# A hybrid attention / RG-LRU block on one core: the opening's loads reordered, weights in 1 KB packets, nine products of zeros first, and the whole order replaced by another

## The chip, the core and the metric

The kernel runs on one core of one Trainium2 chip. Five engines work side by side: TensorE (PE in the views, its weight loads PEld), VectorE (DVE), ScalarE (ACT), GpSimd (POOL) and SyncE (SP), which here issues all DMAs. The metric is the device time of one execution in microseconds. Before the change it is 1078.18 us, the median of 3 runs (1078.18 to 1078.38).

## The reference, cut to what matters

```python
h = rms_norm(x, norm1_g)                      # x: 1024 tokens x 1024
proj = h @ w_in                               # 1024 x 2560: q, k, v, xl, gl, 512 columns each
q, k = rms_norm(q per head), rms_norm(k per head)       # 8 heads of 64
z = q @ k.T / 8                               # causal, strictly below the diagonal
w = sigmoid(z) * prod over later keys of sigmoid(-z)    # stick-breaking weights
attn = w @ v
xl = causal_depthwise_conv(xl)                # 4 taps
lru = rg_lru(xl) * gelu(gl)                   # 2 gates of 8 blocks of 64 x 64, a scan over 1024 tokens
x = x + concat(attn, lru) @ w_out
x = x + square(relu(rms_norm(x) @ w_up)) @ w_down       # 1024 -> 4096 -> 1024
```

## The kernel before, in words

Everything is f32 and held to nearly f32 accuracy by splitting: an operand a becomes a high part (a copy in the reduced f32 format that TensorE takes at full rate, made on ACT) and a low part (a minus the high part, made on DVE or POOL), and a product is three matmuls, low x high, high x low, high x high, added in PSUM.

The program has a front (norm, projections, attention, recurrence, output projection) and an MLP. The MLP saves products by Strassen-like sums of blocks; its matmuls write the banks `p`, `pa`, `pb`, `pc`.

No engine's order is written by hand. `record_front` and `record_mlp` record operations, each with an engine, a cost in ns and the tiles that it reads and writes. The front's operations belong to units, and the string list `ORDER` sets the order of the units: `I` loads the weights `q0` and the transposed input's first half (tokens 0 to 511, `ch` 0), `Xbc` loads two of the eight 128-row blocks (`kc`) of the transposed input (its high and low parts are `hTh` and `hTl`) for half `c`, `Wq1` and the like load weights, `St` loads two 128-token rows of `x` and squares them for the norm, `Rc` spreads the norm's factors over partitions (four transposes into `prs`), `Qpc`, `Vpc`, `Lpc` project, `Gp` normalises q and k (products `ss`, transposes `sst` and `rb`), `Apc` and `Dpc` are attention blocks of head pair p, `B`, `M`, `O`, `U` load and split `w_out` and its input and multiply them, `N`, `H`, `Y`, `Z` prepare the MLP. `Plan.schedule` then plays the recorded operations with a small model of the engines and DMAs, always taking the ready operation with the lowest priority number (the unit's place plus `BIAS` of its kind), and emits them in that order. `ALT` lists, by unit and place in it, the operations that go to their second engine (DVE or POOL, ACT or DVE) instead of their first. So the two tables and `ORDER` settle what stands where in each engine's queue, and an engine runs its queue strictly in that order on the chip.

What the steps below use:

- **The opening.** `xload` loads 128 x 512 of the transposed input, 256 KB, `wload` 128 x 256 of `w_in`, 128 KB. A `q` weight tile holds 128 columns of q and the same 128 of k, which lie 512 columns apart in `w_in`, so each partition gets two pieces of 512 bytes; the `v` tiles are one piece of 1 KB. `q0` uses 8 weight tiles and 8 input tiles for its first half. Each tile goes through ACT (high part: `hTh`, or `wq` with the norm's gain) and DVE or POOL (low part). Then `chain` runs 24 matmuls, 3 for each `kc`, for k and as many for q (`pq001`, `pq000` are k and q of the first half, `pq011`, `pq010` of the second): 48 products of 128x512 for each half.
- **The rows of `x` for the norm** (`sunit`): eight loads of 512 KB into two buffers (tag `A`, `COUNT` 2), squared with a row sum on ACT (`x<-x`, 128x1024), then a few small operations on DVE and a power on POOL (`rstd`).
- **DMA issue.** All loads go through SP in order; eight semaphores (`DMAHW0` to `DMAHW7` in the rows) take turns, so SP issues the ninth load only when the first has landed.
- **The transposes of attention weights**: 128x128 blocks of `w` go through TensorE into `pw`, a PSUM tile of which there is only one (`COUNT` pw=1); ACT or DVE copies it to `wt` before the next four transposes can write `pw`. Then `av` multiplies `wt` with v.
- **The products `w <- w, G`** finish the attention weights (on DVE, or on POOL by `ALT`).
- `warm(n)` existed already but stood in no unit of `ORDER`: n matmuls of a tile of zeros (`zb`, bf16) into a PSUM tile that nobody reads.

Of the kernel before, what the change touches and what calls it, by code (L numbers as in the profile page):

```python
# [1336 lines left out]
```

## Time and profile before

| what | value |
|---|---|
| median of 3 runs | 1078.18 us |
| the profiled execution: its own time | 1078.43 us |
| its span, first to last instruction | 1076.3 us |
| PE busy | 1055.7 us (98%), 5304 matmuls |
| DVE busy | 814.2 us (76%) |
| ACT busy | 575.2 us (53%) |
| POOL busy | 463.4 us (43%) |
| DMA | 120.81 MB, mean 112 GB/s |
| TensorE clock granted, mean | 0.999 |

How to read the views. "busy" is the union of an engine's instructions; a matmul's end is modelled, so neighbours overlap, and what a matmul costs in a dense row is the distance from its start to the next one's. "idle before, releaser" is the time in which the engine did nothing just before an instruction, and what ended it. In a windows view each row gives, for a stretch of the span, the busy time of PE, PEld, DVE, ACT and POOL with their counts, then the granted clock, the share of the DMA engines' time in use, and GB/s. Helper classes issue every instruction, so nearly all rows carry one line number (L1200), and rows are told apart by their tiles: `out<-in`.

### The profile page before, as it was taken

The page shows a single profiled execution, that of the slowest core. Times are in us where ns is not written, and L with a number is a line of the kernel's source. Part 1 is how long each engine was busy: PE and PEld are TensorE (multiplying, and loading weights), DVE is VectorE, ACT ScalarE, POOL GpSimd, SP SyncE. Part 2 cuts the span into 40 slices and gives each one's busy share as a digit, 9 for nine tenths or more (in the row PEclk, how much of TensorE's full clock was granted, in tenths as well). Part 3 has the DMA queues.
Part 4 walks back from the last instruction along what each step waited for, and adds up shares of the span by engine and source line. Part 5 has one row for each costly group of instructions (what it writes and reads, how often), then busy time and mean ns, then how long its engine had stood idle before and what let it go on. Part 6 is the DMA issues. An engine that isn't in the chain of part 4 may idle for free.

```text
span 1076.3 us, 14935 instructions
## 1 busy us (share of the span) xinstructions
PE 1055.7 (98%) x5304; PEld 853.1 (79%) x5304; DVE 814.2 (76%) x1093; ACT 575.2 (53%) x1023; POOL 463.4 (43%) x367
## 2 busy tenths in 40 slices
PE   6999999999999999999999999999999999999998
PEld 4888777769777777788888888888888888888886
DVE  6587877977977885674768888888666659788983
ACT  7754586775576644355227763444443368644431
POOL 2413011113024221267678434557665475742474
PEclk9999999999999999999999999999999999999999
DMA  9402110211117410053443253645343433435662
GB/s 301 155 15 59 31 55 30 64 40 60 33 47 276 164 41 1 21 165 99 135 130 98 89 175 119 186 140 172 105 125 115 129 93 121 117 120 175 199 202 89
DMA packets 80634, 120.81 MB, mean 112 GB/s; under 512 B 9136, under 2 KB 29104, under 8 KB 80560
## 3 DMA queue, kind: packets, MB, share of 16 engines
q1 hardware_dynamic: 80560, 119.86, 35.4%
q8 instruction: 42, 0.69, 0.2%
q14 instruction: 32, 0.26, 0.1%
HBM read 107.77 MB, written 12.06 MB: 111 GB/s over the span
## 4 chain that ended last, share of the span: by engine, by line
PE 90%; DVE 4%; ACT 3%; DMA 2%; issue 1%; SPq 0%; DVEq 0%; ACTq 0%
PE p L1200 28%; PE pa L1200 16%; PE pb L1200 8%; PE po L1200 8%; PE pq L1200 6%; PE pv L1200 4%; PE pc L1200 4%; PE pxl L1200 3%; PE pgl L1200 3%; PE pw L1200 3%; PE av L1200 3%; PE z L1200 2%; ACT x L1200 1%; DMA x<-in_x_dram 1%; DVE G L1200 1%
## 5 line engine op out<-in xcount | busy, mean ns | idle before, releaser
L1200 PE MATMUL pq<-hTh,wq 128*128 128x512 f32 x256 | 87.5, 406 | 11.5 <-DVE wq L1200 9.7
L1200 DVE TENSOR_TENSOR U<-p,U 128x512 f32<-128x512 f32 x80 | 54.7, 687 | 57.4 <-PE p L1200 56.9
L1200 PE MATMUL p<-m1t,st 128*128 128x512 f32 x384 | 89.9, 389 | 0.0
L1200 PE MATMUL p<-m0t,st 128*128 128x512 f32 x384 | 89.7, 389 | 0.0
L1200 PEld LDWEIGHTS p<-m1t,st 128*128 128x128 f32 x384 | 72.0, 188 | 15.1 <-POOL st L1200 0.2
L1200 PEld LDWEIGHTS p<-m0t,st 128*128 128x128 f32 x384 | 72.1, 188 | 14.9
L1200 DVE COPY wt<-pw 128x512 f32<-128x512 f32 (+1 forms) x80 | 50.3, 629 | 29.5 <-PE pw L1200 27.3
L1200 PEld LDWEIGHTS pq<-hTh,wq 128*128 128x128 f32 x256 | 49.1, 192 | 24.6 <-DVE wq L1200 9.7
L1200 PE MATMUL p<-m0b,sb 128*128 128x512 f32 x288 | 67.5, 390 | 0.0
L1200 PE MATMUL p<-m1b,sb 128*128 128x512 f32 x288 | 67.4, 389 | 0.0
L1200 PEld LDWEIGHTS p<-m1b,sb 128*128 128x128 f32 x288 | 54.1, 188 | 11.2
L1200 PEld LDWEIGHTS p<-m0b,sb 128*128 128x128 f32 x288 | 53.9, 188 | 11.1
L1200 ACT ACTIVATE G<-z,qv 128x512 f32<-128x512 f32 (+3 forms) x96 | 49.3, 579 | 25.0 <-PE z L1200 14.1
L1200 ACT ACTIVATE U<-U 128x512 f32<-128x512 f32 x97 | 57.3, 627 | 6.1 <-DVE U L1200 5.2
L1200 ACT ACTIVATE w<-z,qv 128x512 f32<-128x512 f32 (+3 forms) x96 | 48.2, 591 | 17.7 <-PE pw L1200 17.5
L1200 DVE TENSOR_TENSOR_SCAN G<-G,K 128x769 f32<-128x769 f32 (+3 forms) x32 | 47.9, 1507 | 5.4 <-ACT G L1200 4.2
L1200 PE MATMUL pq<-hTl,wq 128*128 128x512 f32 x128 | 50.8, 397 | 0.0
L1200 PEld LDWEIGHTS pw<-ident,w 128*128 128x128 f32 x288 | 34.1, 140 | 20.3 <-DVE wt L1200 6.2
L1200 PE MATMUL pv<-wv,hTh 128*128 128x256 f32 x256 | 49.6, 288 | 0.0
L1200 PE MATMUL pw<-ident,w 128*128 128x128 f32 x288 | 46.1, 278 | 2.3 <-DVE wt L1200 2.3
L1200 POOL MEMSET G<- 128x2 f32 x32 | 3.1, 101 | 104.6 <-DVE w L1200 60.4
L1200 PE MATMUL po<-woh,mxl 128*128 128x512 f32 x112 | 47.0, 420 | 1.0 <-DVE mxl L1200 1.0
(268 smaller groups left out, 2879.2 us busy)
## 6 DMA issues: line engine op xcount, KB each, us to landing
ro<-in_w_out_dram SPq DMA_DIRECT2D x20, 256.0 KB, 5.1
x<-in_xt_dram SPq DMA_DIRECT2D x16, 256.0 KB, 5.2
x<-in_x_dram SPq DMA_DIRECT2D x8, 512.0 KB, 4.9
wrl<-in_w_in_dram SPq DMA_DIRECT2D x32, 128.0 KB, 2.2
x<-in_x_dram SPq DMA_DIRECT2D x16, 256.0 KB, 5.4
b<-in_w_up_dram SPq DMA_DIRECT2D x16, 256.0 KB, 2.8
sa<-in_w_up_dram SPq DMA_DIRECT2D x16, 256.0 KB, 2.7
sb<-in_w_up_dram SPq DMA_DIRECT2D x16, 256.0 KB, 2.7
```

The lines of the kernel that those rows point to most:

```text
L1200: self.last = tc.keep_in_program_order(getattr(self.eng, op)(*args, **kw))
```

## The change

Six things change; the arithmetic of the result does not.

1. `K9` now stands first in `ORDER`: nine matmuls of zeros, 128x512, before the first product.
2. `ORDER`, `ALT` and `BIAS` are replaced by other values, for the front and for the MLP.
3. The columns of `w_in` are permuted in DRAM on the host, so that the 256 columns of every `q` and `l` weight tile lie together: one piece of 1 KB for each partition in place of two of 512 bytes.
4. The model of the DMAs in `Plan.schedule` has other rates and another latency for the first 14 us.
5. The model's latency from PE to another engine goes from 45 to 120 ns.
6. The costs assumed for `z`, `av`, `gm` and the loads of `bd` change. 4, 5 and 6 change nothing in the program by themselves, only what the planner thinks.

```diff
 ORDER = (
-    "B61 C0 Wq1 C1 S3 X11 I X01 S2 S0 X21 Y0 Q00 S1 X31 B51 Q01 Wv0 Q10 R0 V01 Wl3 "
...
+    "K9 C0 X01 B41 B40 X11 Wv0 I Wq1 X21 X31 S2 Wl3 Q00 Q01 Wq2 S1 S3 S0 V01 C1 R0 "
...
-ALT = {"A00": (15, 19, 21,), "A01": (9, 15, 17, 19, 21, 23, 25,), "A02": (9, 15, 22, 28, 32, 36, 39, 41, 43,), "A03": (15, 28, 32, 36, 39, 41, 47,), "A10": (9, 15, 17, 19, 21,), "A11": (9, 17, 21,), "A12": (15, 22, 28, 30, 32, 36, 41,), "A13": (9, 15, 28, 32, 34, 36, 41, 45, 47,),
...
+ALT = {"A00": (17, 19, 21,), "A01": (9, 19, 21, 23,), "A02": (28, 41,), "A03": (15, 32, 34, 36, 45, 47,), "A10": (9, 15, 17, 21,), "A11": (9, 17, 21, 23,), "A12": (9, 22, 28, 30, 34,), "A13": (9, 28, 30, 34, 43,),
...
-                dma_free = x + o.kb * 1024 / 350.0
-                o.end = dma_free + 2000
+                dma_free = x + o.kb * 1024 / (240.0 if x < 6500 else 320.0 if x < 14000 else 350.0)
+                o.end = dma_free + (1600 if x < 14000 else 2000)
...
-                lat = SELF[e] if q.eng == e else 80 if q.eng == "POOL" else 45
+                lat = SELF[e] if q.eng == e else 80 if q.eng == "POOL" else 120 if q.eng == "PE" else 45
...
-            op("SP", 3, ld, w=[(bd, two_)], kb=128, what="bd")
+            op("SP", 3, ld, w=[(bd, two_)], kb=200, what="bd")
...
+        o = 256 * i + {"q": 0, "v": 2 * AW, "l": 3 * AW}[kind]
+
         def ld(wr=wr, rows=rows):
-            if kind == "v":
-                E.sp.dma_start(wr[:, 0:256], rows()[:, 2 * AW + 256 * i:2 * AW + 256 * i + 256])
-            else:
-                o = 0 if kind == "q" else 3 * AW
-                E.sp.dma_start(wr[:, 0:256].rearrange("p (a b) -> p a b", a=2),
-                               rows()[:, o:o + 2 * AW].rearrange("p (a b) -> p a b", a=2)[:, :, P * i:P * i + P])
+            E.sp.dma_start(wr[:, 0:256], rows()[:, o:o + 256])
...
-            cost = sum(3 * MM[kn] + (78 if d else 0) for _, _, kn, d in steps) + 350
+            cost = sum(3 * MM[kn] for _, _, kn, d in steps) + 290
...
-            op("PE", work + 320, mm, r=ws + [VV[p // 2, k] for k in sorted({m // 2 for m in ms})], w=[av], what=f"av{p}{c}", work=work)
+            op("PE", work + 120, mm, r=ws + [VV[p // 2, k] for k in sorted({m // 2 for m in ms})], w=[av], what=f"av{p}{c}", work=work)
...
+        if name == "w_in":
+
+            a = a.reshape(1, 1024, 20, 128)[:, :, [0, 4, 1, 5, 2, 6, 3, 7, 8, 9, 10, 11, 12, 16, 13, 17, 14, 18, 15, 19]].reshape(1, 1024, 2560)
```

What it moves, at three places. First the SP queue at the very start, where `x1_90` is the memory that holds both the input tiles (from `in_xt_dram`) and the `q0` weight tiles (from `in_w_in_dram`), and `x6_193`, `x7_198` are rows of `x` for the norm. Before:

```order
L1200 DMA x1_90<-in_xt_dram 128x512 x5
L1200 DMA vec_71<-in_vecs_dram 128x50
L1200 DMA x1_90<-in_w_in_dram 128x2x128 x5
L1200 DMA x1_90<-in_xt_dram 128x512
L1200 DMA x1_90<-in_w_in_dram 128x2x128
L1200 DMA x6_193<-in_x_dram 128x1024
L1200 DMA x1_90<-in_w_in_dram 128x2x128
L1200 DMA x7_198<-in_x_dram 128x1024
```

Now the same stretch of the SP queue:

```order
L1196 DMA vec_71<-in_vecs_dram 128x50
L1196 DMA x1_90<-in_w_in_dram 128x256
L1196 DMA x1_90<-in_xt_dram 128x512
L1196 DMA x1_90<-in_w_in_dram 128x256
L1196 DMA x1_90<-in_xt_dram 128x512
```

Weights and input now alternate, `vec` (gains and biases) comes first, and no row of `x` stands among them: the first one, `x4`, comes as the 29th load, behind all sixteen input tiles and three `v` weight tiles, in the order x4, x5, x2, x3, x6, x7, x0, x1 (before: x6, x7, x4, x5, x0, x1, x2, x3, and the first was the 14th load).

Second, PE's first products; `hTh` and `hTl` are the input's parts and `wq00`, `wq01` the split weight tiles of `kc` 0 and 1. Before, PE's queue began so:

```order
L1200 MATMUL pq001_217<-hTh_100,wq00_200 128x512
L1200 MATMUL pq001_217<-hTl_101,wq00_200 128x512
L1200 MATMUL pq001_217<-hTh_100,wq00_200 128x512
L1200 MATMUL pq001_217<-hTh_100,wq01_203 128x512
L1200 MATMUL pq001_217<-hTl_101,wq01_203 128x512
L1200 MATMUL pq001_217<-hTh_100,wq01_203 128x512
```

Now PE's queue has the products of zeros ahead (the last of the nine is shown) and goes on so:

```order
L1196 LDWEIGHTS zb_116
L1196 MATMUL warm_169<-zb_116 128x512
L1196 MATMUL pq001_216<-hTh_100,wq00_196 128x512
L1196 MATMUL pq001_216<-hTl_101,wq00_196 128x512
L1196 MATMUL pq001_216<-hTh_100,wq00_196 128x512
L1196 MATMUL pq000_227<-hTh_100,wq00_196 128x512
L1196 MATMUL pq000_227<-hTl_101,wq00_196 128x512
L1196 MATMUL pq000_227<-hTh_100,wq00_196 128x512
```

Each `kc` now serves k and q at once, six products instead of three, until `kc` 4; before, k went through `kc` 0 to 5 before q began. After the 48 products of the second half come two blocks of 12 `pv04` products with the four `ss0` products between them; before, 12 products of `q1` stood between the second half and `ss0`.

Third, PE in attention block 2 of head pair 2, halfway through the front; `pw2210` and the like are uses of the one transpose tile, `w240`, `w250` the attention weights. Before:

```order
L1200 MATMUL pw2210_3410<-ident_63,w250_3363 128x128
L1200 MATMUL po614_3419<-woh41_3160,mxl41_3400 128x512
L1200 MATMUL po614_3419<-wol41_3169,mxh41_3392 128x512
L1200 MATMUL po614_3419<-woh41_3160,mxh41_3392 128x512
L1200 MATMUL po614_3419<-woh51_3113,mxl51_3359 128x512
L1200 MATMUL po614_3419<-wol51_3125,mxh51_3186 128x512
L1200 MATMUL po614_3419<-woh51_3113,mxh51_3186 128x512
L1200 MATMUL pw2211_3443<-ident_63,w240_3348 128x128
```

Now PE has three uses of the tile in a row there:

```order
L1196 MATMUL pw2210_3418<-ident_63,w250_3332 128x128
L1196 MATMUL pw2211_3444<-ident_63,w240_3320 128x128
L1196 MATMUL pw2211_3444<-ident_63,w250_3332 128x128
L1196 MATMUL pw2211_3444<-ident_63,w240_3320 128x128
L1196 MATMUL pw2211_3444<-ident_63,w250_3332 128x128
L1196 MATMUL pw2200_3458<-ident_63,w240_3320 128x128
```

Six output-projection products stood between two uses of `pw`; now nothing does. Over the whole front, before had one such place where a use of `pw` follows another with nothing between (`pw1210`, `pw1211`); now there are four (`pw0320` to `pw0321`, `pw0210` to `pw0211`, `pw2210` to `pw2211`, `pw2211` to `pw2200`). Otherwise PE does the same products as before, and it changes from one kind to another about as often (524 times in the front, was 522).

The new `ALT` also shifts work between DVE and POOL in the front: of the 48 products `w <- w, G`, 24 are on DVE (was 35), and of the 18 of them that were 128x1024 on DVE, 11 remain there; 5 of the 14 `mxl` (was 12), 9 of the 16 `hTl` (was 12) and 9 of the 20 `wol` (was 11) are on DVE. The others are on POOL.

More of the change, by code (lines that the diff above doesn't have):

```diff
@@ L53 @@
 PTAGS = ("z", "pd", "pw", "av")
-ALT = {"A00": (15, 19, 21,), "A01": (9, 15, 17, 19, 21, 23, 25,), "A02": (9, 15, 22, 28, 32, 36, 39, 41, 43,), "A03": (15, 28, 32, 36, 39, 41, 47,), "A10": (9, 15, 17, 19, 21,), "A11": (9, 17, 21,), "A12": (15, 22, 28, 30, 32, 36, 41,), "A13": (9, 15, 28, 32, 34, 36, 41, 45, 47,),
[29 rows of a table removed]
-BIAS = {"vec": -11, "": 27, "x": -9, "hTh": 11, "hTl": 10, "wo": 18, "woh": 3, "wol": 9, "iwq": -14, "iwhq": -25, "iwlq": -30, "ix": -23,
-        "ihTh": -10, "ihTl": -13, "ipq": 16, "sq": -12, "qkh": -30, "qkl": 9, "ipk": -26, "kf": -5, "ssx": 17, "wq": 12, "whq": 18, "wlq": -4,
-        "wv": -5, "whv": 8, "wlv": 30, "pq": 1, "pk": 25, "rsb": 6, "pv": 30, "vh": 11, "wl": 6, "whl": 25, "wll": 30, "ssq": -14,
-        "sse": -11, "sst": 4, "var": 19, "pow": 3, "exp": 20, "rb": 4, "nrm": 10, "nrq": 26, "gm": 5, "z": -3, "sg": -12, "sw": 1,
[3 rows of a table removed]
-        "h": 11, "mvh": -7, "mvl": 2, "nrs": -1, "uap": 30, "uac": -5, "uald": -16, "uash": 26, "uasl": -24, "uar": 15, "uaq": 9, "uh": 15,
-        "uth": 1, "utl": -19, "uvh": -14, "uvl": -3, "uwh": 27, "uwl": 5, "ubld": -30, "usa": -30, "usb": -3, "ubsh": -7, "ubsl": -2, "ubp": -30,
-        "ube": -29, "usc": -23, "uxh": -9, "uxl": -16, "uyh": 30, "uyl": -15, "ucld": 30, "usd": -10, "ucsh": 22, "ucsl": 27, "ucp": 27, "uce": 7,
-        "ucr": -12, "ucq": 1, "dald": 30, "dash": 5, "dasl": 23, "damh": 18, "daml": 8, "dap": -29, "dau": -3, "dav": 30, "dbsh": -6, "dbsl": 26,
-        "dbmh": -26, "dbml": 21, "dbp": -4, "dax": -20, "dbx": -6, "deld": 6, "deu": 25, "dev": 24, "eash": 28, "easl": 2, "eamh": 3, "eaml": 5,
-        "rst": -9, "eap": 28, "ebsh": -22, "ebsl": 9, "ebmh": 10, "ebml": -20, "ebp": 22, "eax": -17, "ebx": -14, "dgld": 30, "dgu": 30, "dgv": 28,
-        "gasl": 1, "gamh": -10, "gaml": -14, "gap": -1, "gcsh": -21, "gcsl": 23, "gcmh": 3, "gcml": 14, "gcp": 28, "gax": -5, "gcx": -6, "dhld": -21,
-        "dhu": 3, "hash": 10, "hasl": 5, "hamh": 2, "hap": -10, "hax": 10, "ubh": -18, "ubl": 14, "out": 5}
@@ new lines @@
+ALT = {"A00": (17, 19, 21,), "A01": (9, 19, 21, 23,), "A02": (28, 41,), "A03": (15, 32, 34, 36, 45, 47,), "A10": (9, 15, 17, 21,), "A11": (9, 17, 21, 23,), "A12": (9, 22, 28, 30, 34,), "A13": (9, 28, 30, 34, 43,),
[28 rows of a table added]
+BIAS = {"warm": -9, "wo": 11, "woh": -6, "wol": -9, "vec": -25, "": 16, "wq": 5, "whq": 16, "wlq": -30, "x": -2, "ssx": -26, "hTh": 18,
+        "hTl": 9, "iwq": -29, "iwhq": -4, "iwlq": -30, "ix": -29, "ihTh": -25, "ihTl": 10, "w_up": 19, "sth": 6, "stl": -26, "ipq": 5, "sq": 2,
+        "qkh": -29, "qkl": -3, "ipk": -17, "kf": -21, "wv": -11, "whv": 11, "wlv": 20, "pq": -24, "pk": 30, "rsb": -26, "pv": -1, "wl": -30,
+        "whl": 5, "wll": -10, "ssq": -14, "sse": -28, "sst": -30, "pow": 13, "exp": 30, "rb": -26, "nrm": -14, "nrq": 30, "bd": -17, "pxl": 5,
[3 rows of a table added]
+        "mvl": -1, "nrs": -26, "uap": 5, "uac": 4, "uald": 18, "uash": 27, "uasl": -18, "uar": 23, "uaq": 2, "uh": 30, "uth": 4, "utl": 9,
+        "uvh": -12, "uvl": -8, "uwh": 10, "uwl": 17, "ubld": -20, "usa": 21, "usb": 1, "ubsh": -10, "ubsl": -17, "ubp": -5, "ube": -9, "usc": 8,
+        "uxh": 9, "uxl": -4, "uyh": -16, "uyl": 12, "ucld": 25, "usd": -4, "ucsh": 11, "ucsl": 23, "ucp": 18, "uce": 27, "ucr": 3, "dald": 24,
+        "dash": -22, "dasl": 5, "damh": 3, "daml": -15, "dap": -5, "dau": -30, "dav": 18, "dbsh": -7, "dbsl": 7, "dbmh": -8, "dbml": 30, "dbp": 20,
+        "dax": 30, "dbx": 8, "deld": -30, "deu": 28, "dev": 23, "eash": -4, "easl": -13, "eamh": 3, "eaml": 27, "rst": -29, "eap": -24, "ebsh": -2,
+        "ebsl": -3, "ebmh": -11, "ebml": -30, "ebp": -24, "eax": 29, "ebx": 12, "dgld": 7, "dgu": 26, "dgv": 24, "gash": 14, "gasl": 7, "gamh": -22,
+        "gaml": -9, "gap": -8, "gcsh": -14, "gcsl": 26, "gcmh": -9, "gcml": 27, "gcp": 14, "gax": -19, "gcx": 1, "dhld": -19, "dhu": 4, "hash": -20,
+        "hasl": -17, "hamh": -22, "haml": -7, "hap": -6, "hax": 12, "ubh": 1, "ubl": 24, "out": 10}
@@ L737, in bound @@
                         E.gps.memset(two(G, kn + 1)[:, :, kn:kn + 1], 0.0)
-                    op("POOL", 200, bound, w=[(G, "b")], what=f"gm{p}{c}", port=False)
+                    op("POOL", 160, bound, w=[(G, "b")], what=f"gm{p}{c}", port=False)
             def burst(steps=steps, zs=zs):
@@ L747, in burst @@
                             E.pe.matmul(z[:, h, :kn], q[hs, a, cols], k[hs, b, :kn], start=n == 0, stop=n == 2)
-            cost = sum(3 * MM[kn] + (78 if d else 0) for _, _, kn, d in steps) + 350
+            cost = sum(3 * MM[kn] for _, _, kn, d in steps) + 290
             rd = [QH[p, r // 4, 0] for r, _, _, _ in steps[:1]] + [QH[p, steps[0][1] // 512, 1]]
-            op("PE", cost, burst, r=rd, w=list(zs.values()), what=f"z{p}{c}", work=cost - 350)
+            op("PE", cost, burst, r=rd, w=list(zs.values()), what=f"z{p}{c}", work=cost - 290)
             for (r, k0, kn, diag) in steps:
```

75 rows, old and new, of tables (ALT, BIAS, ORDER) are left out of this document.

## The prediction

> **What bounds the kernel now.** I read the page first, then the windows, then PE's waits, then the start of the timeline. The page, with busy times and shares of the span:
>
> ```profile
> span 1076.3 us, 14935 instructions
> ...
> PE 1055.7 (98%) x5304; PEld 853.1 (79%) x5304; DVE 814.2 (76%) x1093; ACT 575.2 (53%) x1023; POOL 463.4 (43%) x367
> ```
>
> PE is the bound, and what a reordering can win is at most what PE does not do at full pace. The windows say where that is:
>
> ```profile
> 0.00:9.70 9.70, 0.00 (x0) 0.00 (x0) 5.32 (x12) 5.54 (x10) 3.27 (x14) 1.00 0.78 232
> 9.70:13.30 3.60, 3.59 (x9) 2.82 (x10) 3.00 (x10) 1.95 (x5) 0.00 (x0) 1.00 0.94 303
> 13.30:27.00 13.70, 12.81 (x56) 10.30 (x55) 9.89 (x26) 12.85 (x25) 3.94 (x4) 1.00 1.05 349
> 27.00:54.00 27.00, 26.84 (x150) 21.95 (x149) 15.69 (x49) 18.90 (x39) 11.43 (x10) 1.00 0.48 154
> ```
>
> For 9.7 us PE does nothing. Then nine products take 3.6 us (0.40 each), though the clock column says 1.00; from 13.3 to 27 it is 56 in 12.81 us, 0.23 each. The DMA engines are busy all the while (0.78, 0.94, 1.05). The last part, the MLP, has nothing to win:
>
> ```profile
> 463.50:1072.00 608.50, 608.50 (x2685) 503.44 (x2683) 463.55 (x543) 289.97 (x507) 357.02 (x246) 1.00 0.43 133
> ```
>
> 608.5 busy of 608.5. Between lies the front; PE's waits, with who ended them, total, times, longest:
>
> ```profile
> PE pq L1200 <- DVE wq L1200: 9.7, 1, 9.7
> PE pw L1200 <- DVE wt L1200: 2.3, 3, 1.1
> PE po L1200 <- DVE mxl L1200: 1.0, 1, 1.0
> PE pq L1200 <- DVE q L1200: 0.9, 1, 0.9
> PE pq L1200 <- ACT x L1200: 0.9, 1, 0.9
> PE pxl L1200 <- DVE q L1200: 0.7, 1, 0.7
> PE ht L1200 <- DVE h L1200: 0.6, 2, 0.4
> PE pxl L1200 <- ACT x L1200: 0.3, 1, 0.3
> PE prs L1200 <- DVE qv L1200: 0.2, 1, 0.2
> ```
>
> After the first row only 6.9 us remain, 5.7 of them on DVE. So three things can move the time: the opening (9.7 us, 1.5 us of slow pace, and the 0.9 us of the fourth row), these waits, and new ones.
>
> **The opening: how early the products can end.** The first matmuls and the hole in them:
>
> ```profile
> 9.71 0.79 PE L1200 MATMUL pq<-hTh,wq 128*128 128x512 f32 x1 [9.71 <-DVE wq L1200]
> ...
> 24.32 0.39 PE L1200 MATMUL pq<-hTh,wq 128*128 128x512 f32 x1
> 25.60 0.51 PE L1200 MATMUL pq<-hTh,wq 128*128 128x512 f32 x1 [0.89 <-DVE q L1200]
> ```
>
> Counting the order up to this hole, 57 products are done when the 58th starts at 25.60. The new opening is set by data. The bytes that moved, in slices of 1 us from 0 to 40, and the first load with its first user:
>
> ```profile
> GB/s 0 27 272 309 145 260 329 340 339 312 264 334 303 337 362 392 410 396 360 285 258 373 354 354 357 305 350 413 375 425 188 205 176 353 237 311 234 155 132 0
> ```
>
> ```profile
> 0.73 2.29 SPq L1200 DMA_DIRECT2D x<-in_xt_dram  x5
> ```
>
> ```profile
> 3.50 0.62 ACT L1200 CAST hTh<-x 128x512 fp32r<-128x512 f32 x1 [1.49 <-DMA x<-in_xt_dram]
> ```
>
> An issue takes 0.46 us (2.29 for 5), and a 256 KB load is usable 2.8 us after its issue. The first input tile is now third in the queue: usable at about 4.4. ACT's and DVE's pieces:
>
> ```profile
> L1200 ACT CAST hTh<-x 128x512 fp32r<-128x512 f32 x16 | 9.5, 617 | 3.8 <-DMA x<-in_xt_dram 3.6
> L1200 ACT ACTIVATE x<-x 128x1024 bf16<-128x1024 f32 x8 | 8.4, 1056 | 2.9 <-DMA x<-in_x_dram 2.8
> ...
> L1200 ACT ACTIVATE sq<-pq 128x512 f32<-128x512 f32 x6 | 3.6, 596 | 2.2 <-PE pq L1200 2.1
> ```
>
> Weight first (0.5), then `hTh` (0.6): the first product starts near 5.2, the second only with `hTl` near 6.6. That is not what decides: the 48 products of the first half need everything up to the eighth pair, 25 KB + 8 x 384 KB + 2 x 128 KB of `v` weights = 3.35 MB. The slices reach 3.23 MB at 13.0 and 3.57 at 14.0, so it has moved at 13.4, is usable at 13.9, and cast and subtraction (0.6 and 0.7, ACT a little behind) end near 15.3. Eleven of the 48 products are then left, at 0.227: they end at 17.9, and the 57th at 20.0. Against 25.6 that is a **lead of 5.6 us**. Bounds: ready a microsecond earlier or later, 4.5 to 6.5. The 1 KB packets concern 1.05 MB of this; at 303 GB/s (window row 9.7 to 13.3) or 349 (13.3 to 27) that differs by 0.46 us, taken as 0.
>
> **The nine products of zeros** read a tile that DVE fills early:
>
> ```profile
> 0.89 0.27 DVE L1239 MEMSET zb<- 128x256 uint32 x1
> ```
>
> It is ready at 1.16, and nine at 0.40 to 0.43 run to about 5.0, all in PE's empty start, before the first real product. They cost nothing, and they pay for the 1.5 us that nine products lost at the slow pace. Since data decides above, that gain is already in the 5.6. The Trainium skill ("TensorE: Matmul & The Clock Gate", Part 1) has the full clock come after one busy window of about 3.4 us whose start is not tied to the program; the 3.6 us row agrees. By that rule nine products could straddle two windows and open neither; the sum would then be 1.5 us worse (rival E).
>
> **What the lead loses again.** Three places. (a) The 58th to 60th products need the fourth input tile of the second half, cast and subtracted at about 20.3 by the same count: 0.3 us. (b) `ss0` squares the second half. It waits for `sq010`, and before, twelve more `pq` products stood between; now only twelve `pv04` of 0.12, 1.4 us. The 96 products end at 28.9, PE is at `ss0` at 30.3. On ACT two squares of rows (1.06 each), `sq011`, the cast and `sq010` (0.6 each) queue up there: done at 30.4 if the rows come early, 31.5 if they come when I reckon. I take 1.2. (c) `prs0` needs the norm's factors of all first-half rows, and the last rows of `x` are now loaded later:
>
> ```profile
> x<-in_x_dram SPq DMA_DIRECT2D x8, 512.0 KB, 4.9
> ```
>
> ```profile
> 18.36 0.55 SPq L1200 DMA_DIRECT2D x<-in_x_dram  x1
> ...
> 23.99 0.38 SPq L1200 DMA_DIRECT2D x<-in_x_dram  x1
> ...
> 27.25 0.34 SPq L1200 DMA_DIRECT2D x<-in_x_dram  x1
> ...
> 31.07 0.34 SPq L1200 DMA_DIRECT2D x<-in_x_dram  x1
> ...
> 32.67 0.96 SPq L1200 DMA_DIRECT2D x<-in_x_dram  x1
> ```
>
> ```profile
> L1200 POOL TENSOR_TENSOR rstd<-var,mhalf 128x2 f32<-128x2 f32 x4 | 2.8, 703 | 15.9 <-DVE var L1200 14.9 <-DVE sp__113 L1200 1.1
> ```
>
> Two buffers take turns. The six loads from 18.36 to 32.67 make two and a half turns, 5.7 us each. The first row load now is the 29th and waits for the landing of the 21st, which ends 3.74 MB: 15.0. Three turns later 32.1, its partner 1.2 behind at 33.3, landing 4.9 later at 38.2, square, sums, power (1.06 + 0.4 + 0.70): 40.4. PE is at `prs0` after 32.6 us of products at the dense pace, plus 7.0 (17.9 less the first 48's 10.9), plus 1.5 for (a) and (b), plus 0.5 for changes of product: 41.6. So 0, with 1.2 us to spare; with turns of 7.1 us, as the one from 23.99 to 31.07, it stalls 3.0 (rival C). The lead that stays: 5.6 - 0.3 - 1.2 = **4.1 us**, bounds 1.0 to 6.
>
> **New waits at the transposes.** With one `pw` tile, a use right behind another waits for its copy. Before has one such place:
>
> ```profile
> 229.46 0.60 PE L1200 MATMUL pw<-ident,w 128*128 128x128 f32 x4
> 231.19 0.66 PE L1200 MATMUL pw<-ident,w 128*128 128x128 f32 x4 [1.13 <-DVE wt L1200]
> ```
>
> 1.13 us. The new order has four: **3 x 1.13 = 3.4 us lost**, bounds 2.0 (where PE would wait for something else anyway) and 5 (DVE busy when the copy is due).
>
> **The other waits.** Without that pair, PE waits for DVE after 27 us: 2.3 - 1.1 + 1.0 + 0.7 + 0.6 + 0.2 = 3.7 us. DVE gets less to do in the front:
>
> ```profile
> L1200 DVE TENSOR_TENSOR w<-w,G 128x1024 f32<-128x1024 f32 x18 | 23.6, 1322 | 1.9 <-ACT w L1200 1.5
> ...
> L1200 DVE TENSOR_TENSOR mxl<-rm,mxh 128x512 fp32r<-128x512 f32 x12 | 9.5, 791 | 2.1 <-ACT mxh L1200 1.4 <-PE z L1200 0.6
> ```
>
> ```profile
> L1200 POOL TENSOR_TENSOR w<-w,G 128x1024 f32<-128x1024 f32 x6 | 13.8, 2304 | 24.5 <-DVE G L1200 15.1 <-ACT w L1200 9.4
> ```
>
> Seven wide products (9.3 us) and seven `mxl` (5.5 us) leave it. I take half of the 3.7 us as gone, **1.8 us**; bounds 3.7 gone, or 3 more where a late POOL product (2.3 us for 1.3) is what PE waits for. The MLP, with PE at 100% and DVE and POOL below 80%, gets 0; its cover is that slack, and a stall there would show as the first wait of PE after 463 us.
>
> **Sum.** -4.1 + 3.4 - 1.8 = -2.5 us on the profiled 1078.43 (span 1076.3 and 2.1 around it): 1075.9. The median is 0.25 lower, so I forecast **1075.7**. About 0.2% (2.2 us) is what a measurement here can tell from no change: faster means below 1076.0, slower above 1080.3.
>
> **Rivals.** *B, the waits are better than the rows allow:* the full lead and all 3.7 us gone: -5.6 - 3.7 + 3.4 = -5.9, 1072.3. For it: DVE's relief, 14.8 us, is four times these waits. Against: the four DVE waits of 0.6 to 1.1 us stand where a copy or a low part is on the way to PE, and such places the new order has as well.
>
> *C, the rows of `x` become the bound of the opening:* turns of 7.1 us put the power at 44.6, `prs0` stalls 3.0, and the sum is +0.5: 1078.7. For it: one of the turns above was that long. Against: the other was 5.4 (27.25 to 32.67), and fewer loads compete there now.
>
> *D, slower, POOL holds DVE:* seven more wide products on POOL take 16.1 us and free 9.3 on DVE. If DVE's own two-input work stands still meanwhile, DVE loses 6.8 us net in a front where it is 80% busy. With the other waits unchanged the sum stands at -0.7, so PE need pay only 2.9 of these 6.8 to end slower; with half, 3.4, it is 1080.9. For it a middle stretch (DVE third, POOL fifth), and the products on DVE (min/median/max):
>
> ```profile
> 140.00:240.00 100.00, 96.97 (x536) 74.22 (x534) 80.09 (x112) 73.91 (x125) 16.79 (x25) 1.00 0.14 44
> ```
>
> ```profile
> L1200 DVE TENSOR_TENSOR w<-w,G x35: 410/1214/2135, 60.9 to 425.5; 128x1024 f32<-128x1024 f32 x18, 128x512 f32<-128x512 f32 x7, 128x768 f32<-128x768 f32 x7, 128x256 f32<-128x256 f32 x3
> ```
>
> The longest took 2135 ns, 0.8 us over the mean of the widest, 1322. Against: POOL was busy for 16.8 of those 100 us and has room, and the copies out of PSUM that PE waits for read no second tile. The Trainium skill ("SBUF — State Buffer", SBUF: two separate sides) says that DVE instructions with two SBUF inputs and POOL instructions take turns on a shared port pair, the loser blocked for the whole instruction; the 2135 ns agrees, but the row does not show what POOL did then.
>
> *E, the zeros open no window:* +1.5, 1077.2.
>
> **How the numbers follow.** Forecast 0.42 (faster 0.30, same 0.12 by its bounds), B 0.15 (faster), C 0.20 (same 0.14, slower 0.06), D 0.15 (slower 0.14, same 0.01), E 0.08 (same 0.06, faster 0.02). Faster 0.47, same 0.33, slower 0.20. The range runs from a little under B to D with half paid, 1071.0 to 1081.0; left out are the far ends of B and D. The forecast's own range, 1073 to 1077.5, holds only its case.
>
> **What would show it.** PE's first product of data between 4.8 and 6, the last of the first 48 at 17 to 19, and no pair of products at 0.40 us after 7. A wait of `ss` for ACT near 30 of about 1 us, none at `prs`. Three to four waits of `pw` for `wt` of 1 us more than before, and `mxl`, `q` and `h` smaller. Wrong would be: a first half that ends after 20, `prs` waiting over 2 us, DVE's mean for `w<-w,G` 128x1024 above 1.6 us, or any wait in the MLP.

## The result, and the profile after

The changed kernel takes 1085.79 us, the median of 5 runs (1084.43 to 1087.01); the kernel before, on the same chip, 1078.18 (5 runs, 1077.85 to 1081.45). The ratio is 1.0064, with a 95% interval of 1.0047 to 1.0081: **slower by 7 us, where 2.5 us faster was forecast**, and outside the range. The profiled execution took 1085.82 us, with a span of 1084.0.

The page of after, span and busy times:

```profile
span 1084.0 us, 14954 instructions
...
PE 1063.9 (98%) x5313; PEld 852.5 (79%) x5313; DVE 796.4 (73%) x1074; ACT 576.3 (53%) x1024; POOL 491.0 (45%) x385
```

DVE does 18 us less than before, POOL 28 more, ACT the same. The windows that the prediction cut, now:

```profile
0.00:9.70 9.70, 7.63 (x22) 3.47 (x22) 8.08 (x28) 5.58 (x10) 3.29 (x14) 1.00 0.67 209
9.70:13.30 3.60, 3.51 (x14) 2.66 (x15) 3.25 (x9) 3.23 (x8) 1.34 (x2) 1.00 1.07 369
13.30:27.00 13.70, 12.78 (x54) 9.54 (x53) 9.51 (x17) 12.20 (x24) 8.12 (x7) 1.00 0.99 328
27.00:54.00 27.00, 25.31 (x167) 21.85 (x166) 12.44 (x42) 17.44 (x35) 10.00 (x9) 1.00 0.52 164
```

PE works from the start, and the stretch from 9.7 to 13.3 has 14 products where there were 9. But from 27 to 54 PE is busy for 25.31 us, where it was 26.84. PE's longest waits in after and the one in the MLP (total, times, longest):

```profile
PE pw L1196 <- DVE wt L1196: 6.5, 9, 1.1
PE pxl L1196 <- ACT x L1196: 2.3, 3, 1.0
PE pv L1196 <- ACT sq L1196: 1.7, 1, 1.7
PE warm L1196 <- DVE ones L1236: 1.2, 1, 1.2
PE pq L1196 <- ACT sq L1196: 0.8, 1, 0.8
PE sst L1196 <- ACT sq L1196: 0.7, 1, 0.7
PE av L1196 <- DVE wt L1196: 0.7, 1, 0.7
...
PE pb L1196 <- DVE x L1196: 0.4, 1, 0.4
```

The wait of 9.7 us for the first weights is gone; those for the copy of the transposes (`wt`) have grown from 2.3 to 6.5 us.

**Where the time went.** For every matmul I take the distance to the next one's start less the dense pace of its form, and add these up. Up to 27 us PE had lost 12.7 us in before and 8.9 in after (the zeros not counted as work): a lead of 3.85 us. From 27 us on it loses 47.5 us in before and 59.1 in after: 11.55 more. 11.55 less 3.85 is 7.7 us, the whole difference. By kind of product, the 11.55 are: transposes right behind transposes +2.7, `pv` +2.55, `pg` (the gates) +2.0, `pxl` +1.9, `av` +1.6, transposes behind other work +1.4, and the rest together -0.6, with +0.5 for the MLP among them. So the question for the runs is what the 11.55 are, and whether the 3.85 are real.

How such a wait comes about, at 113 to 118 us of after, PE first:

```profile
113.38 0.66 PE L1196 MATMUL pw<-ident,w 128*128 128x128 f32 x4 [1.02 <-DVE wt L1196]
114.03 1.20 PE L1196 MATMUL pg<-x,bd 64*128 64x512 f32 x4
116.28 0.66 PE L1196 MATMUL pw<-ident,w 128*128 128x128 f32 x4 [1.05 <-DVE wt L1196]
```

and DVE over the same stretch:

```profile
112.64 0.67 DVE L1196 COPY wt<-pw 128x512 f32<-128x512 f32 x1
113.24 0.73 DVE L1196 SCALAR_TENSOR_TENSOR x<-x,vec,pxl 128x512 f32<-128x512 f32 x1
113.90 1.75 DVE L1196 TENSOR_TENSOR_SCAN G<-G,K 128x769 f32<-128x769 f32 x1
115.57 0.66 DVE L1196 COPY wt<-pw 128x512 f32<-128x512 f32 x1
```

The transposes of 113.38 are done at 114.0. Their copy stands in DVE's queue behind a scan that began at 113.90 and takes 1.75 us; it runs at 115.57, and PE, whose queue has the next transposes at its head, waits 1.05 us. At 161 us two scans (2.45 us) stand ahead of such a copy, at 178 us one of 2.28.

### The profile page after: what moved, and what is told of

It reads as the page before. It is cut to its first block, busy times and chain, and to the rows that moved or that the text cites. A ratio compares the mean times of both kernels' runs of the same rounds, so it can differ in the third digit from the quotient of the medians.

```text
span 1084.0 us, 14954 instructions
## 1 busy us (share of the span) xinstructions
PE 1063.9 (98%) x5313; PEld 852.5 (79%) x5313; DVE 796.4 (73%) x1074; ACT 576.3 (53%) x1024; POOL 491.0 (45%) x385
## 2 busy tenths in 40 slices
DMA packets 72443, 120.82 MB, mean 111 GB/s; under 512 B 9136, under 2 KB 20912, under 8 KB 72368
## 4 chain that ended last, share of the span: by engine, by line
PE 86%; DVE 6%; ACT 3%; DMA 3%; issue 2%; SPq 0%; DVEq 0%; ACTq 0%
PE p L1196 28%; PE pa L1196 16%; PE pb L1196 8%; PE po L1196 7%; PE pq L1196 5%; PE pc L1196 4%; PE pv L1196 4%; PE pxl L1196 3%; PE pgl L1196 3%; PE av L1196 2%; PE pw L1196 2%; PE z L1196 2%; DVE x L1196 2%; DVE G L1196 1%; ACT x L1196 1%
## 5 line engine op out<-in xcount | busy, mean ns | idle before, releaser
L1196 POOL TENSOR_TENSOR w<-w,G 128x1024 f32<-128x1024 f32 (+3 forms) x24 | 40.7, 1701 | 109.1 <-ACT w L1196 69.4
L1196 DVE COPY wt<-pw 128x512 f32<-128x512 f32 (+1 forms) x80 | 50.3, 629 | 32.5 <-PE pw L1196 28.7
L1196 PEld LDWEIGHTS pq<-hTh,wq 128*128 128x128 f32 x256 | 48.1, 188 | 13.3 <-ACT sq L1196 1.3
L1196 DVE TENSOR_TENSOR_SCAN G<-G,K 128x769 f32<-128x769 f32 (+3 forms) x32 | 50.2, 1574 | 7.7 <-ACT G L1196 7.6
L1196 POOL TENSOR_TENSOR U<-U 128x512 f32<-128x512 f32 x28 | 37.4, 1337 | 26.4 <-DVE sdb L1196 11.6
```

The source lines that it names most:

```text
L1196: self.last = tc.keep_in_program_order(getattr(self.eng, op)(*args, **kw))
```

## The experiments

Eighteen kernels, each measured next to the kernel before on the same chip; five chips served, and the kernel before had medians between 1078.35 and 1079.29 us on them. So between runs on different chips the ratios compare better than the times. "Loss behind 27 us" is the sum defined above, taken from the profiled execution. Every kernel does the whole computation.

Some runs keep or splice an order. There the program is emitted by a given rank of every operation, lowest ready rank first, in place of the planner's priorities; a rank read off a kernel's own order gives that kernel's queues again.

```diff
-    plan.schedule()
+    plan.follow({o.key: n for n, o in enumerate(order)})
```

### Parts of the opening undone

**e1, no zeros.**

```diff
-    "K9 C0 X01 B41 B40 X11 Wv0 I Wq1 X21 X31 S2 Wl3 Q00 Q01 Wq2 S1 S3 S0 V01 C1 R0 "
+    "C0 X01 B41 B40 X11 Wv0 I Wq1 X21 X31 S2 Wl3 Q00 Q01 Wq2 S1 S3 S0 V01 C1 R0 "
```

> The changed kernel without its nine products with zeros; every other instruction keeps its place. Theory O (the order behind 27 us costs 11.5 us, the opening's lead of 3.9 us is real): the zeros only open the clock, so without them some of the first 48 products run at the slow pace while the loads still hold them back: between 1085.8 and 1087.5 us (the 9 to 16 slow products of 0.21 us more each, partly under waits for loads). Theory Z (the zeros delay the opening or the first copies): 1083 to 1085 us. If the zeros do nothing at all: 1085.8 us within 0.5.

Measured: 1085.42 us (1084.34 to 1087.77), ratio 1.006 (1.0047 to 1.0074). The zeros do what they are for and it is worth nothing. Without them PE's first products are at the slow pace (two in 0.86 us at 7.02, two in 0.45 from about 9.5 on):

```profile
5.35 0.79 PE L1368 MATMUL pq<-hTh,wq 128*128 128x512 f32 x1 [5.35 <-ACT hTh L1368]
6.43 0.79 PE L1368 MATMUL pq<-hTl,wq 128*128 128x512 f32 x1 [0.29 <-DVE hTl L1368]
7.02 1.05 PE L1368 MATMUL pq<-hTh,wq 128*128 128x512 f32 x2
...
9.96 0.40 PE L1368 MATMUL pq<-hTl,wq 128*128 128x512 f32 x1
```

and yet PE has lost 8.65 us by 27 us, against 8.9 with them: the products catch up with the loads and wait for those in both kernels.

**e2, pieces of 512 bytes.** The old layout and load of `w_in`, in the changed order.

```diff
-            E.sp.dma_start(wr[:, 0:256], rows()[:, o:o + 256])
+                E.sp.dma_start(wr[:, 0:256].rearrange("p (a b) -> p a b", a=2),
+                               rows()[:, o:o + 2 * AW].rearrange("p (a b) -> p a b", a=2)[:, :, P * i:P * i + P])
```

> The changed kernel with w_in in its old layout and loaded in pieces of 512 bytes; the order of all instructions is the changed one. Theory O: packets are worth at most 0.5 us, 1085.8 to 1086.3 us. If the larger packets carry the opening's lead: up to 3.9 us slower, 1088 to 1090 us; the first 96 products would then end near 34 us and not 30.8.

Measured: 1084.71 us (1083.23 to 1086.32), ratio 1.005 (1.0037 to 1.0063). The larger packets are worth nothing here: 80,635 of them in place of 72,443, and the loss by 27 us is 9.1, not 8.9.

### The changed opening before the old order

**e3, first splice.** The changed order and choices up to the 96th product, those of before from there on.

```diff
+    first = new[:new.index(("V01", 1))]
+    rank = {k: n for n, k in enumerate(first + [k for k in old if k not in first])}
```

> The changed kernel's order (zeros, loads, choice of engines) up to its 96th product of the opening, and from there on the order and the choice of engines of the kernel before. Theory O, and theory P (products moved to POOL behind the opening cost the time) alike: the lead of 3.9 us stays, 1074.3 us (1073.5 to 1076). If an earlier opening is taken back by the later stages whatever their order, 1077.5 to 1078.5 us. If the opening itself does harm (tiles or loads left in a worse state), above 1079 us.

Measured: 1104.57 us (1104.06 to 1105.29), ratio 1.0233 (1.0219 to 1.0246). None of the theories had this. PE's waits in e3:

```profile
PE pq L1372 <- DVE wq L1372: 12.0, 4, 7.6
PE ss L1372 <- ACT sq L1372: 9.9, 1, 9.9
```

The changed opening loads v's weights next, since its order goes on with `pv`; the old order goes on with `q1`, whose weights and rows of `x` now stand behind them. Transposes and `av` lose what they lose in before, to 0.1 us (10.88 us against 10.90, 13.74 against 13.75); of the others `pxl` loses 0.7 us more and `po` 1.2 less. So the loss sits where the two orders are joined: in this splice the 3.85 us of lead cannot be cut off from the loads that they push back.

**e7, second splice.** Only what leads to the 96 products is taken over, with all other loads behind it in the old order.

```diff
+    todo = [o.key for o in new if o.what == "warm" or o.eng == "PE" and o.key[0] in ("Q00", "Q01")]
+        if k not in seen:
+            seen.add(k)
+            todo.extend(deps.get(k, ()))
```

> The kernel before with only what leads to the first 96 products taken over from the changed kernel (the zeros, the loads of those products and of the weights in 1 KB packets, their casts and their order), every other load directly behind those and in the order of before; behind that the order and the choices of before. Theory O: the stages behind 27 us take what they took before (47.5 us of loss), the opening keeps its lead of 3.9 us: 1074.3 us (1073.5 to 1075.5). If what leads is paid by the loads and squares that now come later (a wait at the sums of squares or at the weights of the next product, as in the first splice): 1077 to 1082 us, with that wait in the list.

Measured: 1086.92 us (1086.75 to 1089.52), ratio 1.0079 (1.0066 to 1.0091). One wait of 8.4 us in the opening (`pq` for DVE's `t_c`, ending at 22.6 us): a four-element step of the recurrence's constants stands on DVE ahead of the weights' low parts and waits for ACT, which waits for rows of `x` that now come later. Behind 27 us the loss is 50.3 where before has 47.5, and 2.2 of the 2.8 more are at `pq`: the old order stays itself.

**e12, third splice.** As e7, with that chain taken over as well (units `C0`, `C1`) and each operation behind the loads that it waits for.

```diff
-    todo = [o.key for o in new if o.what == "warm" or o.eng == "PE" and o.key[0] in ("Q00", "Q01")]
+    todo = [o.key for o in new if o.key[0] in ("K9", "C0", "C1") or o.eng == "PE" and o.key[0] in ("Q00", "Q01")]
...
+        t = max([o.start] + [end[k] for k in deps.get(o.key, ())])
```

> The splice of before's order behind the changed opening once more, with what held it up mended: the small chain from the lambda of the recurrence taken over from the changed kernel too, and each instruction of before's that waits for a load that now comes later put behind it. Theory O and theory M: no wait over 2 us left in the first 30 us, the lead of 3.9 us stays, 1074.3 us (1073.5 to 1076). If the lead is lent (the loads of the rows of x and of the second weights come later and their users wait): 1077 to 1081 us.

Measured: 1082.59 us (1081.46 to 1084.8), ratio 1.0045 (1.0032 to 1.0058). Now the first 27 us are those of after (8.9 lost), and the old order pays at 33 to 51 us:

```profile
33.41 0.50 PE L1396 MATMUL pq<-hTh,wq 128*128 128x512 f32 x1 [2.56 <-ACT f L1396]
45.32 0.40 PE L1396 MATMUL prs<-ident,rstd 128*128 128x128 f32 x2 [1.77 <-DVE qv L1396]
46.54 0.43 PE L1396 MATMUL prs<-ident,rstd 128*128 128x128 f32 x2 [0.82 <-POOL rstd L1396]
51.09 0.66 PE L1396 MATMUL rb<-ident,sq 128*128 128x128 f32 x4 [2.71 <-ACT sq L1396]
```

7.9 us in four waits, for squares and rows whose loads were put off. So in this splice too the old order pays for the lead later. That no splice could keep it is not shown.

### The choice of engines

**e4 and e5.** The changed order with before's choices between DVE, ACT and POOL in the front, and the reverse; 125 operations of the front differ.

```diff
+    PICK = lambda k: k[1] in (mlp if k[0][0] == "m" else front).get(k[0], ())     # front: the other kernel's ALT
```

> The changed kernel's order, but in the front end every choice between DVE, ACT and POOL as in the kernel before (125 instructions of the front change engine; the MLP keeps the changed choices). Theory P (the products moved to POOL hold DVE, which then gives out the copies late): most of the 11.5 us comes back, 1074.5 to 1079 us, and the mean of DVE's 128x1024 products falls back from 1.53 to about 1.32 us. Theory O: the order sets the losses whoever computes, 1083 to 1088 us, with the four back-to-back uses of the transposes' tile still at 3.4 us.

> The kernel before, order and loads untouched, but in the front end each choice between DVE, ACT and POOL as in the changed kernel (125 instructions change engine, the MLP keeps its own). On the changed order the changed choices were worth 2.8 us (1085.8 against 1088.6). Theory E (the choices are worth that on any order): 1075 to 1076.5 us. Theory F (choices only fit the order they were searched with): 1079 to 1083 us. Theory P (products on POOL hold DVE): above 1081 us, with late copies in the waits for the transposes' tile.

Measured: e4 1088.58 us (1086.42 to 1090.58), ratio 1.0085 (1.0071 to 1.0099); e5 1083.86 us (1083.12 to 1084.49), ratio 1.0045 (1.0033 to 1.0057). With the two kernels this is a square; loss behind 27 us:

| | before's choices | changed choices |
|---|---|---|
| before's order | 47.5 | 52.1 |
| changed order | 58.4 | 59.1 |

Down a column, the order costs 7.0 to 10.9 us; along a row, the choices cost 4.6 or 0.7 (e4 also loses 1.1 us more in the opening than after does). So rival D (POOL holds DVE) is not what made the kernel slower: with its products back on DVE the changed order is no faster. e5 is less clear: 1083.86 us lies 0.9 above theory F and in the range of theory P, but P's sign, more late copies, is missing (PE waits 2.3 us in 3 for them, as in before). What the 4.6 us are there stays open. What rival D rests on is there, though. DVE's widest `w<-w,G` in after and in e4, count, busy, mean ns:

```profile
L1196 DVE TENSOR_TENSOR w<-w,G 128x1024 f32<-128x1024 f32 x11 | 16.9, 1533 | 0.3
```

```profile
L1370 DVE TENSOR_TENSOR w<-w,G 128x1024 f32<-128x1024 f32 x18 | 23.0, 1276 | 0.7 <-ACT w L1370 0.4
```

With 24 of the 48 products on POOL one on DVE takes 0.26 us longer than with 13 there. The Trainium skill ("SBUF — State Buffer", SBUF: two separate sides) has DVE instructions with two SBUF inputs and POOL's wait for each other; these rows fit that, without showing what POOL did meanwhile, and the 11 products are not the same mix as the 18. On eleven instructions that is 2.8 us of DVE, and PE did not wait for those.

**e8, the second splice with the changed choices everywhere**, the MLP's too.

```diff
+    PICK = lambda k: k[1] in new_alt.get(k[0], ())
```

> The spliced kernel (opening of after, order of before) with the changed kernel's choices between DVE, ACT and POOL everywhere, in the MLP too. Theory E: another 2.8 us below the splice, about 1071.5 us. Theory F: 1 to 5 us above the splice. Theory P: 3 to 11 us above the splice.

Measured: 1098.86 us (1097.63 to 1098.97), ratio 1.0182 (1.0169 to 1.0195), 12 us above the splice, more than theory F (1 to 5) or P (3 to 11) allowed: 3.2 us more between 27 and 470 us (4.2 in e5), and 7.4 in the MLP, whose old order meets choices made for another. On before's order the changed choices do harm in both parts; theory E is out.

### Single waits

**e6, the pairs apart.**

```diff
+    for k, place in [(("Q10", 8), ("A03", 35)), (("A02", 33), ("A01", 3)),
+                     (("A22", 33), ("Q30", 11)), (("U61", 2), ("A22", 38))]:
+        rank[k] = rank[place] - 0.5
```

> The changed kernel with one piece of PE's work put between each of the four neighbouring pairs of transposes (at 68, 112, 334 and 336 us); all else in place. Theory O: three to four of the waits of 0.79 to 1.02 us go, and nothing else comes late: 1085.8 less 2.2 to 3.4, so 1082.4 to 1083.6 us. Theory L (DVE is late with its copies wherever the transposes stand, the waits only move): 1085 to 1086.5 us.

Measured: 1084.85 us (1084.55 to 1088.07), ratio 1.0064 (1.0049 to 1.0078). At the pairs 2.0 us went, a little less than expected; 0.8 came back at other transposes, 0.9 at `pq`. Between the two theories, and not the main thing.

### Who copies the transposes

The front section says that ACT or DVE copies `pw` to `wt`, as the plan does. The rows say otherwise. DVE's copies in after:

```profile
L1196 DVE COPY wt<-pw 128x512 f32<-128x512 f32 (+1 forms) x80 | 50.3, 629 | 32.5 <-PE pw L1196 28.7 <-PE av L1196 3.2
```

and in before:

```profile
L1200 DVE COPY wt<-pw 128x512 f32<-128x512 f32 (+1 forms) x80 | 50.3, 629 | 29.5 <-PE pw L1200 27.3 <-PE av L1200 1.7
```

All 80 are on DVE, and ACT has none, though by `ALT` 39 belong to ACT in after and 32 in before. The reason is a name. `op` keeps the chosen engine in `e` for the function that will issue the instruction, and further down a loop over the PSUM banks uses `e` again. The loop runs only for operations that touch the tiles `z`, `pd`, `pw` or `av`; each of those with a choice between ACT and DVE finds that `e` is not `"ACT"`, and issues on DVE. The plan, its times and its order go on counting on ACT.

**e9 and e10: the name mended**, in after and in before.

```diff
-                    for e, d in v.bank.items():
-                        if e[0] == b and e[1] != eng:
+                    for held, d in v.bank.items():
+                        if held[0] == b and held[1] != eng:
```

> The changed kernel with one loop variable renamed in the planner's recording of an operation. As it stands, that loop overwrites the name of the chosen engine for every operation that touches the PSUM tiles z, pd, pw or av, and each such copy that has a choice is issued on DVE, though the order is planned with 56 of the front's copies on ACT (39 of the 80 copies behind the transposes, 10 of v, 7 of the attention's output); in the kernel before it is 43. Renamed, the copies run where the plan has them; nothing else changes. Theory M (the changed order loses because more of its copies run on an engine that it did not count on, behind scans): the late copies at 115, 161, 178 and 377 us go, PE's loss behind 27 us falls from 59 us to 45 to 52 us, DVE's busy time by about 32 us: 1072 to 1079 us. Theory O (the order itself, whoever copies): 1083 to 1088 us.

> The kernel before with the same one name mended: 43 copies go from DVE to ACT (32, 7 and 4). Theory M: it gains as well, less than the changed kernel since fewer copies move and its order was chosen by what ran: 1072 to 1078 us, and the gap between the two kernels shrinks to under 4 us or turns. Theory O: the gap of 7 to 8 us stays. If ACT's copies hold up its own work (the sigmoids, the squares): above 1079 us.

Measured: e9 1078.92 us (1076.8 to 1081.11), ratio 1.0006 (0.9997 to 1.0015); e10 1077.42 us (1076.16 to 1079.61), ratio 0.9995 (0.9986 to 1.0004). The gap between the two orders falls from 7.6 to 1.5 us. Loss behind 27 us: 52.0 in e9 (59.1 in after), 46.0 in e10 (47.5 in before). The waits in e9:

```profile
PE pw L1196 <- DVE wt L1196: 2.4, 3, 0.8
PE pxl L1196 <- ACT x L1196: 2.3, 3, 1.0
PE pv L1196 <- ACT sq L1196: 1.3, 1, 1.3
...
PE pw L1196 <- ACT wt L1196: 0.7, 1, 0.7
```

What is left at `pw` are the four pairs. The six lone waits for a copy in after (at 80, 115, 161, 178 and 279 us before transposes, at 377 before `av`; 3.8 us in all) are gone, and every one of these six copies is ACT's in the plan. The copies of e9 on its two engines:

```profile
L1196 DVE COPY wt<-pw 128x512 f32<-128x512 f32 (+1 forms) x41 | 25.8, 630 | 25.3 <-PE pw L1196 20.4 <-PE av L1196 4.4
```

```profile
L1196 ACT COPY wt<-pw 128x512 f32<-128x512 f32 (+1 forms) x39 | 21.3, 546 | 42.6 <-PE pw L1196 42.4
```

And the place shown above, now on ACT, where the copy of 112.90 follows its transposes at once while DVE runs two scans:

```profile
111.37 0.59 ACT L1196 COPY wt<-pw 128x512 f32<-128x512 f32 x1 [0.70 <-PE pw L1196]
111.85 1.17 ACT L1196 ACTIVATE G<-z,qv 128x384 f32<-128x384 f32 x2
112.90 0.60 ACT L1196 COPY wt<-pw 128x512 f32<-128x512 f32 x1
```

**e11, the plan told the truth instead**: those kinds of copy are planned on DVE, the tables stay, the order comes out anew.

```diff
-            if self.inunit in ALT.get(self.uname, ()):
+            if self.inunit in ALT.get(self.uname, ()) or (eng, alt[0]) == ("ACT", "DVE"):
```

> The changed kernel whose planner is told the truth: the four kinds of copy are planned on DVE, where they do run, and the order comes out anew from the same tables. The work of each engine is that of the changed kernel. Theory M: the order now makes room on DVE for the copies, the late ones behind scans go: 1076 to 1083 us. Theory O, or if the tables only fit the order that they were searched with: 1084 to 1092 us.

Measured: 1129.25 us (1125.2 to 1130.37), ratio 1.0465 (1.0447 to 1.0483), with waits everywhere (`pw` for `wt` 11.6 us in 14, `pv` for ACT 4.6, `sst` 3.9). Outside what either theory allowed. So the run is no test of the copies. That tables chosen for one set of costs give a poor order with another would explain it; no run shows that.

**e13 and e14: which copies.** Only those behind the transposes as planned, then all but those.

```diff
-            f, e = fn, eng
-            fn = lambda: f(e)
+            f, run = fn, "DVE" if what.startswith(("vh", "ob", "h2")) else eng     # e14: what.startswith("wth")
+            fn = lambda: f(run)
```

> The changed kernel where of the copies with a choice only those behind the transposes run as planned (39 go to ACT); those of v, of the attention's output and of h stay on DVE as they ran. Theory M with the transposes' tile as its place: most of the 6.9 us, 1079 to 1081.5 us. If the 25 others carry it: 1083 to 1086 us.

> The counterpart: the copies of v, of the attention's output and of h run as planned (25 go to ACT), the 80 behind the transposes all stay on DVE. Theory M with the transposes' tile as its place: 1083.5 to 1086 us. If the others carry it: 1079 to 1081 us. If DVE's total load is what counts, in proportion to the time moved (about 11 of 32 us): 1083.5 us.

Measured: e13 1078.22 us (1076.48 to 1080.44), ratio 0.9997 (0.9988 to 1.0006); e14 1087.0 us (1086.51 to 1087.71), ratio 1.0077 (1.0063 to 1.0091). The 39 copies behind the transposes carry all of it, 7.6 us; the other 25 bring nothing (1.2 us above after). By kind of product, e13 loses 8.6 us less behind 27 us than after, and 6.3 of these are at the transposes and at `av`, which use the copies. e14 also tells what about them counts. Its page:

```profile
PE 1065.3 (98%) x5313; PEld 854.1 (79%) x5313; DVE 785.0 (72%) x1049; ACT 586.2 (54%) x1049; POOL 489.2 (45%) x385
```

DVE has 11 us less to do than in after, about half of the 23 us less in e13 (773.2), and the time is no better. So it is not DVE's load, but where the copies of the single tile stand in its queue.

### What is left

**e15 and e16**, on the mended kernel e9: the pairs apart and two squares of `x` on ACT put behind the squares of the product that `pv` waits for; then also two transposes ahead of the products that wait behind the gates.

```diff
+    for k, place, off in PAIRS + [(("S1", 2), ("Q01", 9), 0.3), (("S1", 4), ("Q01", 9), 0.4)]:
+        rank[k] = rank[place] + off
+    # e16: (("A12", 31), ("L11", 1), -0.5), (("A21", 16), ("L21", 1), -0.5)
```

> The mended changed kernel (copies as planned, 1078.9 us) with the four pairs of transposes apart, and the two squares of x rows on ACT behind the first product's squares at 31 us. Theory W (what is left are single places in the list of waits): 2.1 us for three pairs and 1.3 us for the square go, 1075.0 to 1077.0 us. Theory O (the waits move): 1078 to 1080 us.

> As the last, and two transposes drawn ahead of the product that waits right behind the gates (0.91 and 0.97 us at 220 and 268 us). Theory W: another 1.3 to 1.9 us, 1073.5 to 1075.5 us. Theory O: no faster than the last, since the transposes then wait for what they transpose.

Measured: e15 1080.49 us (1079.21 to 1082.13), ratio 1.0013 (1.0004 to 1.0022); e16 1080.79 us (1078.69 to 1081.6), ratio 1.0015 (1.0006 to 1.0024). Neither is faster than e9 (the intervals overlap). In e15 the transposes behind transposes lose 1.84 us less and the `pv` wait of 1.3 us is gone, but `pv` waits 1.3 us for its weights, whose high parts now stand right behind those squares on ACT, and `sst` 1.9 for ACT. In e16 the edit did not reach its place: the two transposes came forward by one product, not ahead of the one that waits, because the tiles they need come free only there; the wait behind the gates is what it was (2.3 us in 3). So single places can be emptied, but e15 shows such a wait moving on, and whether the gates' 2.3 us can be had stays open.

**e17 and e18**: the pairs apart alone, on e13; and e13's mending in the kernel before (32 copies to ACT).

```diff
+    for k, place in PAIRS:       # the four of e6
+        rank[k] = rank[place] - 0.5
```

> The kernel of e13 (only the transposes' copies as planned, 1078.2 us) with the four pairs of transposes apart and nothing else. Theory W (single waits are what is left): 1.84 us less behind pw and 0.58 more at pw, so 1.3 us: 1076.5 to 1077.3 us. Theory O (the waits move, as the 0.9 us at pq in e15): 1077.8 to 1079 us.

> The kernel before where of the copies with a choice only those behind the transposes run as planned (32 to ACT). Theory M: as e10, 1077 to 1078 us, since its waits for such copies come to 2.3 us only; the gap to e13 (1078.2) is then under 1.5 us, and the two orders are alike within 0.15%. If the 11 others cost in e10 what they seem to cost between e9 and e13 (0.7 us): 1076.5 us.

Measured: e17 1076.92 us (1075.67 to 1078.31), ratio 0.9989 (0.998 to 0.9998); e18 1077.26 us (1076.28 to 1078.8), ratio 0.9993 (0.9983 to 1.0002). With their copies where they were planned, the two orders are alike. The median of e17 is 1.3 us below e13's, which would be theory W, but their intervals overlap, and the profiled executions are only 0.2 us apart (1076.82 and 1077.05): there the pairs lose 1.8 us less, while a wait of `pq` for ACT of 1.3 us stands that e13 does not have, and `pv` loses 0.7 more. So between theories W and O this stays open. e17 is the only one of the eighteen whose interval lies below the kernel before, by 0.1%.

## Why the prediction was wrong

- **The opening.** First and second product at 5.34 and 6.43 (5.2 and 6.6 forecast), the last of the first 48 at 18.49, so they end at 18.7 (17.9). A lead of 3.85 us at 27 where 5.3 was forecast; a wait of 0.84 us for ACT at 19.7, which the sum did not have, is part of that, and 0.2 is a slip: its loads are in KB of 1024 bytes, so 3.43 MB had to move, not 3.35, and the slices reach that at 13.6, not 13.4. Right in kind, 1.4 too good.
- **Zeros and packets at nothing.** Right, for the reason given (e1, e2). Rival E falls twice: behind the zeros the products run at 0.23 us wherever they do not wait, and e1, which has the slow ones, is no slower. The Trainium skill ("TensorE: Matmul & The Clock Gate", Part 1) has the full clock come after some 3.4 us of work; e1's rows agree roughly: slow from 5.35 to about 9.5 us, 4.1 us with pauses.
- **The loss (b), 1.2 us at `ss0`.** It came as 1.67 us one step earlier, at the `pv` ahead of `ss0`, which needs the PSUM tile that ACT empties only behind a square of `x`. Mechanism right, place and size a little off. **(c) and rival C:** no wait of `prs` is in after's list; right.
- **Transposes.** Four pairs at 0.79, 1.02, 0.79 and 0.78 us, 3.37 in all and 2.24 more than before's 1.13; forecast 3.4. Right by the rule, a third less in size. The 1.13 us that the forecast took for a pair were themselves a wait for a copy that the plan has on ACT (in e10, where it runs there, that wait is 0.7).
- **The other waits, 1.8 us gone "through DVE's relief": this is the step that failed.** It took DVE's total as what sets these waits, and -1.8 us became about +7.6. In the prediction's terms the 7.7 us are -3.85 (lead) + 1.67 (b) + 2.24 (pairs) + 7.6 (these). The relief came (814.2 to 796.4 us busy), and the waits in the list, pairs and opening apart, went from about 4 us up to about 8, with 3.6 us more in pauses that are too short or too mixed for the list. e14 shows that less work on DVE does not help by itself, e13 that 39 copies do: with them on ACT that part of the list is back at about 4 us. The plan put these on ACT, 7 more than in the kernel before (32), and in the order that it made they stand on DVE behind scans and other work. Counting rows by engine would have shown it beforehand: before's trace has 80 copies on DVE and none on ACT.
- **Why before suffered so little** from the same fault, 0.9 to 1.2 us (e10, e18) and not 7.6, is only argued: it may have been kept for what it measured, and so have its copies where DVE has room. That was not tried. The fault shows there too: 2.1 of its 2.3 us of waits at `pw` are for copies that its plan has on ACT.
- **The MLP at 0.** It lost 0.5 us, with a wait of 0.4 for DVE at 671 us. Any wait there was to be a sign of being wrong; it came, and it is small. **Rival D:** e4 and e5 above.

What stays open: the mended orders tie (e13 and e18, 1078.2 and 1077.3), although one has a lead of 3.85 us at 27 us. In e13's list stand 3.0 us at the pairs, 0.9 at `pv` and 2.2 behind the gates, together more than the lead; no run shows clear of noise that any of it can be had back. So even with the copies in place the 2.5 us of the forecast do not appear.

## What to carry to other kernels

Before you reason about an order, count in the trace which engine each planned operation ran on; a plan that is wrong there cannot be read from its tables. An engine's load says little about waits for a single buffer: ask what stands ahead of the copy that frees it, in that engine's queue, and how long that takes. And a lead at the start is worth only as much as the loads that it put off can wait for.
